# Feed-forward block in two phases through HBM: the first product for all pairs, then the second product with seven block products for eight

## The chip, the cores and the metric

The kernel runs on one core of a Trainium2 chip. A core has TensorE (matrix products, written PE; its weight loads PEld), VectorE (DVE), ScalarE (ACT), GpSimd (POOL) and SyncE (SP), which here issues nearly all transfers (DMAs) between the device memory, HBM, and the on-chip memory, SBUF. Products are summed up in PSUM, eight banks of 128 x 512 float32. The metric is the device time of one execution in microseconds (us).

## What is computed

One layer of a decoder trunk on 1024 tokens of width 1024, in float32. After a mixing part (four groups of token mixers and an output projection) comes the feed-forward block, which the change is about:

```python
    h = h + mixed @ w_out[l]
    f = jnp.square(jax.nn.relu(rms_norm(h, ffn_norm_g[l]) @ w_ff1[l]))   # 1024 -> 4096
    h = h + f @ w_ff2[l]                                                 # 4096 -> 1024
return rms_norm(h, final_norm_g)
```

## The kernel before

**Products in three passes.** Each float32 operand is split into a rounded high part and a low rest (`split`: ScalarE copies and rounds the high part, VectorE subtracts it). A product is three matmuls, high by high, high by low and low by high (`mm3`). `split_to` splits a 128 x 512 piece into one tile of two halves.

**Pairs.** The 4096 columns of the inner layer are taken in 16 pairs of 128-column tiles (`NPAIR`). For a pair, the first product is a matrix of 2 x 2 blocks: two tiles of inner columns by two halves of 512 tokens, summed over two halves of the width. `ff1_pair` computes it with seven block products for eight (Strassen's scheme in Winograd's form): VectorE makes sums of the weight blocks `a11` to `a22`, `mm_half` is one block product of 12 matmuls of 128 x 512, and the banks `ffx`, `ffy`, `ffz`, `ffv` collect them. The operands of the token side (`hb`: `B11`, `B21`, `T1`, `B22`, `T2`, `T3`, `T4`) are made once: `hn_T0` transposes the first half of the tokens, `hn_T1` the second and forms the first sums, `combine_2` and `combine_3` the rest. `add_relu2` adds, applies the squared ReLU and splits the result into `f`.

**Second product.** `ff2` runs right behind, pair by pair and half by half: for each of four token tiles, 2 tiles of inner columns x 2 halves of 512 output columns x 3 passes, 96 matmuls a pair for both halves; `done` adds the result, times the row's norm `rs2`, into `h` on VectorE (128 x 1024). Its weights come through `load_w2`: four pieces of 256 KB a pair through one buffer (tag `e`), each split into `w2h` and `w2l`.

**The first pair** is done in another way (`boot_w`, `boot_t1`, `boot_t2`): eight plain block products, the four of the first token half ahead of `hn_T1`, so that TensorE has work while the second half of the tokens is still being normed and transposed. `h_norm` norms the tiles of `h`: two squares of 512 columns on ScalarE, an addition and a power on GpSimd, a scaling on ScalarE. It is called for the tiles 0 to 3 after the attention's last `attend` of that half, and for 6, 7, 5, 4 after `att_tile(4)`.

**Order.** The program's order and the priorities in it (`tc.high_priority`) are turned by a scheduler into one fixed order for each engine; an instruction or a load goes ahead of its place when its buffers are free in the scheduler's model. At run time each engine, and SP's queue of transfers, works its list strictly in order. Buffers are rings by tag: `w` has ten tiles of 4 KB a partition (split weights), `raw` two (loaded weights), `M` two, `N` and `e` one, `A` eight (the tiles of `h`), `B` eight, `O`, `P`, `K`, `V`, `Z` four each. In PSUM `X` is two tiles of two banks, `W` two banks, `K` and `O` one each.

**The end.** `final` norms a tile of `h` and stores it; the last tile (`final_tile`) goes in pieces of 512, 256 and 256 columns.

## Time and profile before

| | |
|---|---|
| three runs | 1107.32, 1104.01, 1103.83 us; median 1104.01 |
| the profiled execution | 1102.54 us; its span from first to last instruction 1100.8 us |
| mean clock granted to TensorE | 0.979 |
| moved by DMA | 64.99 MB, mean 59 GB/s |
| from the start to 390 us | mixing part, attention, output projections |
| 390 to 455 us | end of the attention, first pair, `hn_T1`: TensorE busy 57.03 of 65.00 us |
| 455 to 1041 us | loop over pairs: TensorE busy 586.00 of 586.00 us, VectorE 384.99, ScalarE 163.98 |
| 1041 to 1101 us | last pair and end: TensorE busy 43.38 of 60.00 us |

How to read the profile: a row of the page's groups gives line, engine, operation, out <- in by the program's names, how often, then busy time and the mean duration of one in ns, then the idle time of the engine before these and what ended it. In the tables by stage a row is a stretch of the span, its length, and the busy us (and number of instructions) of PE, PEld, DVE, ACT, POOL, then the granted clock, the DMA engines' share and GB/s. Matmuls overlap, so the duration of one is more than the time from one to the next.

### The profile page before, as it was taken

To read this page: it belongs to the slowest core of one execution; us is meant where nothing else is said; L and a number is where in the kernel's file an instruction comes from. 1 tells how busy PE (TensorE), PEld (TensorE's weight loads), DVE (VectorE), ACT (ScalarE), POOL (GpSimd) and SP (SyncE) were. 2 spreads that over 40 slices of the span, in tenths; PEclk is the share of its full clock that TensorE was granted. 3 is DMA by queue.
4 is the path that set the end of the run, shared out by engine and by line. 5 is a ranking of instruction groups with operands and counts; after the bars stand their busy time and mean duration, and the time that the engine had idled before them with its cause. 6 is when DMAs were issued, how large, how long until landed. Compare 5 with 4: busy or idle time off the path is not lost.

```text
span 1100.8 us, 12943 instructions
## 1 busy us (share of the span) xinstructions
PE 1042.1 (95%) x4870; PEld 858.5 (78%) x4870; DVE 800.8 (73%) x1096; ACT 430.1 (39%) x805; POOL 174.7 (16%) x217
## 2 busy tenths in 40 slices
PE   9986799999999697999999999999999999999986
PEld 7865688888888585788888888888888888888765
DVE  5999998998797348975667666567567567567557
ACT  7551266546566656241332222322322322322223
POOL 0468756114233210000000000000000000000003
PEclk9998899999999799999999999999999999999998
DMA  9311025011000000121211201202202202202103
GB/s 342 138 51 46 20 71 201 29 39 39 2 22 19 0 7 14 48 67 48 67 41 37 77 18 60 77 10 68 77 10 67 77 10 67 77 10 87 39 29 152
DMA packets 24973, 64.99 MB, mean 59 GB/s; under 512 B 2768, under 2 KB 4688, under 8 KB 24912
## 3 DMA queue, kind: packets, MB, share of 16 engines
q1 hardware_dynamic: 24768, 64.11, 17.2%
q8 instruction: 38, 0.62, 0.2%
q14 instruction: 23, 0.19, 0.1%
q10 hardware_dynamic: 144, 0.07, 0.0%
HBM read 59.97 MB, written 4.19 MB: 58 GB/s over the span
## 4 chain that ended last, share of the span: by engine, by line
PE 74%; DVE 15%; ACT 4%; issue 3%; DMA 3%; POOL 1%; SPq 0%; POOLq 0%; DVEq 0%; ACTq 0%
PE ff L159 29%; PE ffx L159 11%; PE ffy L159 7%; DVE acc L336 7%; PE wo L159 4%; PE ffv L159 4%; PE ffz L159 4%; PE ob L159 2%; PE s L675 2%; PE zc L159 2%; PE zml L159 2%; PE ffb L159 2%; PE woa L159 2%; DMA w_raw<-in_w_ff 1%; PE ptb L718 1%
## 5 line engine op out<-in xcount | busy, mean ns | idle before, releaser
L159 PE MATMUL ff<-w2h,f 128*128 128x512 f32 (+1 forms) x1024 | 336.8, 392 | 11.8 <-ACT w2h L129 4.1
L159 PEld LDWEIGHTS ff<-w2h,f 128*128 128x128 f32 x1024 | 192.3, 188 | 56.8 <-ACT w2h L129 5.4
L949 DVE SCALAR_TENSOR_TENSOR h<-ff,rs,h 128x1024 f32<-128x1024 f32 x127 | 162.1, 1281 | 93.6 <-PE ff L159 92.2
L159 PE MATMUL ff<-w2l,f 128*128 128x512 f32 x512 | 200.2, 391 | 0.0
L159 PE MATMUL ffx<-hnT,w1s 128*128 128x512 f32 x540 | 139.8, 392 | 0.0
L129 ACT ACTIVATE w1s<-w_raw 128x512 fp32r<-128x512 f32 x107 | 67.1, 629 | 159.0 <-PE ffy L159 50.1
L159 PEld LDWEIGHTS ffx<-hnT,w1s 128*128 128x128 f32 x540 | 101.4, 188 | 22.6
L159 PEld LDWEIGHTS ff<-w2l,f 128*128 128x128 f32 x512 | 96.4, 188 | 21.2 <-DVE w2l L130 0.8
L981 POOL TENSOR_SCALAR mr_ms<-mssq,epsr 128x1 f32<-128x1 f32 x7 | 2.7, 392 | 670.5 <-ACT fjunk L979 670.5
L129 ACT ACTIVATE w2h<-w_raw 128x512 fp32r<-128x512 f32 x64 | 40.4, 632 | 163.4 <-PE ff L159 100.2
L130 DVE TENSOR_TENSOR w1s<-w_raw,w1s 128x512 fp32r<-128x512 f32 x107 | 73.3, 687 | 34.4 <-ACT w1s L129 33.0
L336 DVE SCALAR_TENSOR_TENSOR acc<-ycv,cols,acc 128x512 f32<-128x512 f32 (+23 forms) x100 | 96.3, 1002 | 0.8 <-ACT acc L316 0.6
L130 DVE TENSOR_TENSOR w2l<-w_raw,w2h 128x512 fp32r<-128x512 f32 x64 | 44.1, 689 | 65.4 <-ACT w2h L129 65.0
L129 ACT ACTIVATE f<-s 128x512 fp32r<-128x512 f32 x60 | 37.6, 628 | 99.3 <-PE ff L159 59.5
L159 PE MATMUL ffz<-hnT,w1s 128*128 128x512 f32 x180 | 46.7, 393 | 0.0
L130 DVE TENSOR_TENSOR f<-s,f 128x512 fp32r<-128x512 f32 x60 | 41.1, 684 | 7.0 <-ACT f L129 6.8
L159 PE MATMUL ffy<-hnB,w1s 128*128 128x512 f32 x180 | 45.4, 390 | 0.0
L159 PE MATMUL ffv<-hnT,w1s 128*128 128x512 f32 x180 | 44.9, 390 | 0.0
L159 PE MATMUL ffy<-hnT,w1s 128*128 128x512 f32 x180 | 44.5, 393 | 0.0
L159 PEld LDWEIGHTS ffz<-hnT,w1s 128*128 128x128 f32 x180 | 33.8, 188 | 7.8
L159 PEld LDWEIGHTS ffy<-hnT,w1s 128*128 128x128 f32 x180 | 33.8, 188 | 7.7
L849 DVE SCALAR_TENSOR_TENSOR s<-s 128x512 f32<-128x512 f32 x60 | 39.7, 683 | 0.1
(441 smaller groups left out, 1952.0 us busy)
## 6 DMA issues: line engine op xcount, KB each, us to landing
w_raw<-in_w_ff SPq DMA_DIRECT2D x64, 256.0 KB, 2.7
w_raw<-in_w_ff SPq DMA_DIRECT2D x32, 512.0 KB, 4.0
xin<-in_x SPq DMA_DIRECT2D x8, 512.0 KB, 8.4
wo_raw<-in_w_out SPq DMA_DIRECT2D x8, 512.0 KB, 3.6
h<-in_x SPq DMA_DIRECT2D x8, 512.0 KB, 5.7
out<-h SPq DMA_DIRECT2D x7, 512.0 KB, 2.6
xraw<-in_xT SPq DMA_DIRECT2D x8, 256.0 KB, 4.5
xraw<-in_xT SPq DMA_DIRECT2D x4, 512.0 KB, 9.0
```

The lines of the kernel that those rows point to most:

```text
L129: act.activation(h, src, AF.Copy)
L130: dve.tensor_sub(l, src, h.bitcast(F32))
L159: pe.matmul(out, lhs(x), rhs(y), start=start and i == 0, stop=stop and i == 2, skip_group_check=more)
L336: dve.scalar_tensor_tensor(aa, ya, c, aa, ALU.mult, ALU.add)
L675: pe.matmul(sb_[:, c0:c0 + w], q[:, x, qo:qo + P], kt[:, y, 0:w], start=i == 0, stop=i == 2 and not last)
L718: pe.transpose(b[:, place[j] + s * P:place[j] + (s + 1) * P], pts[s][:, (2 * kp + j) * P:(2 * kp + j + 1) * P], ident)
L849: dve.scalar_tensor_tensor(s, s, 0.0, s, ALU.max, ALU.mult)
L949: dve.scalar_tensor_tensor(h[t], banks[t], rs2[:, t:t + 1], h[t], ALU.mult, ALU.add)
L981: pool.tensor_scalar(ms, ssq, 1.0 / D, epsr[:, t:t + 1], ALU.mult, ALU.add)
```

## The change

The feed-forward block is taken apart into three steps. (1) `early(p)`, for pairs 0 to 9: the two block products that need only the first half of the tokens (`B11`, `B21`), 24 matmuls. The first is stored to HBM (`m1`), their sum gives a quarter of `f`; `hn_T1`, `combine_2` and `combine_3` are laced in between. (2) `ff1_pair(p)` for all 16 pairs: pairs 0 to 9 load their first product back and copy it into PSUM, and do the other five block products; pairs 10 to 15 do all seven. Pair 0 is now a pair like the others. `f_out` stores each quarter of `f` to HBM in float32 (`fr`), and three of four also split (`fs`). (3) `ff2_chunk(c)`, four chunks of four pairs: the second product as 2 x 2 blocks (two halves of the tokens, two tiles of inner columns, two halves of the output) with seven block products for eight. A block product (`product`) is 4 token tiles x 4 pairs x 3 passes = 48 matmuls; banks `A` (both `X` tiles) and `B` (`W`, `W`, `K`, `O`) collect them, and after each `add_h` adds the 128 x 512 result to its place in `h`. The sums of the blocks of `f` and `w_ff2` are made by VectorE before products 3 and 4. The operands of products 1, 2 and 7 (`f_load`) come split from HBM into the ring `B`, the others are split from the raw `f` in `K` and `O`; the raw weights lie in `Z` and `P`, the split ones in `w`. `att_h` norms each tile of `h` right behind its `att_tile`, with one square of 1024 columns.

```diff
     with (
...
+        tc.tile_pool(name="hbm", bufs=1, space=bass.MemoryType.DRAM) as hbm,
...
-    ssh = const([P, 2 * NT], "ssh")
+    ssh = const([P, NT], "ssh")
...
     def h_norm(t):
-        for n in range(2):
-            jk = M("hjunk", [512])
-            act.activation(jk, h[t][:, n * 512:(n + 1) * 512], AF.Square, accum_out=ssh[:, n * NT + t:n * NT + t + 1])
-        ms = small(1, "gssq")
-        pool.tensor_tensor(ms, ssh[:, t:t + 1], ssh[:, NT + t:NT + t + 1], ALU.add)
-        power(rs2[:, t:t + 1], ms, 1, "gr", 1.0 / D, nhalf)
+        jk = M("hjunk", [512]).bitcast(BF16)
+        act.activation(jk, h[t], AF.Square, accum_out=ssh[:, t:t + 1])
+        power(rs2[:, t:t + 1], ssh[:, t:t + 1], 1, "gr", 1.0 / D, nhalf)
         act.activation(h[t], h[t], AF.Copy, scale=rs2[:, t:t + 1])
-    HF = (0, 1)
+    def att_h(t):
+        att_tile(t)
+        h_norm(t)
...
+    NEARLY = 10
+    NCH = 4
...
-    def load_w2(p):
...
-    def add_relu2(f, b, s):
...
-    def ring():
...
-    def boot_w():
...
-    def boot_t1():
...
-    def boot_t2():
...
+    def E(name):
+        return sb.tile([P, 512], F32, tag="e", name=name, bufs=1)
+    def dram(name, n, dt=F32):
+        return hbm.tile([P, n], dt, tag=name, name=name, bufs=1)
+    fr = [[dram("fr%d_%d" % (p, i), 1024) for i in range(2)] for p in range(NPAIR)]
+    fs = [{q: dram("fs%d_%d" % (p, q), 1024) for q in (0, 1, 3)} for p in range(NPAIR)]
+    m1 = [dram("m1_%d" % p, 512) for p in range(NEARLY)]
+    def f_out(p, q, b, s, f, stage):
+        dve.tensor_add(f, b, s)
+        dve.scalar_tensor_tensor(f, f, 0.0, f, ALU.max, ALU.mult)
+        nc.sync.dma_start(fr[p][q // 2][:, (q % 2) * 512:(q % 2 + 1) * 512], f)
+        if q != 2:
+            t = split_to(stage("fst"), f)
+            nc.sync.dma_start(fs[p][q], t.rearrange("p x c -> p (x c)").bitcast(F32))
+    def load_w1(p, i):
+        return load_raw(a["w_ff1"][2 * p + i], 1024, "w1_raw")
+    def early(p):
+        ra = load_w1(p, 0)
+        w11 = split_to(slot("w1e"), ra[:, 0:512])
+        w12 = split_to(slot("w1e"), ra[:, 512:])
+        b = W("ffe")
+        mm_half(b, w11, "B11", True)
+        s1 = M("s1e", [512])
+        act.activation(s1, b, AF.Copy)
+        nc.sync.dma_start(m1[p], s1)
+        b = W("ffe")
+        mm_half(b, w12, "B21", True)
+        f_out(p, 0, b, s1, (E, N)[p % 2]("fe"), lambda n: sb.tile([P, 2, 512], F32R, tag="CS", name=n, bufs=1))
     def ff1_pair(p):
-        ra, rb_ = load_w1(p)
+        ra, rb_ = load_w1(p, 0), load_w1(p, 1)
         a11, a12, a21, a22 = ra[:, 0:512], ra[:, 512:], rb_[:, 0:512], rb_[:, 512:]
-        w11 = split_to(ring(), a11)
+        b = X("ffxy")
+        bx, by = b[:, 0:512], b[:, 512:]
+        s1 = E("s1")
+        if p < NEARLY:
+            nc.sync.dma_start(s1, m1[p])
+            if p < 2:
+                pe.matmul(bx, hb["B11", 0][:, 0, 0:P], hb["B11", 0][:, 0, :], start=True, stop=True)
+            act.activation(bx, s1, AF.Copy)
+        else:
+            w11 = split_to(slot("w1s"), a11)
         dve.tensor_add(a21, a21, a22)
         dve.tensor_sub(a11, a21, a11)
-        ws1 = split_to(ring(), a21)
-        bx, by = W("ffx"), K("ffy")
-        mm_half(bx, w11, "B11", True)
-        s1 = M("s1", [512])
-        act.activation(s1, bx, AF.Copy)
+        ws1 = split_to(slot("w1s"), a21)
+        if p >= NEARLY:
+            mm_half(bx, w11, "B11", True)
+            act.activation(s1, bx, AF.Copy)
         mm_half(by, ws1, "T1", True)
         s5 = N("s5")
         act.activation(s5, by, AF.Copy)
-        ws2 = split_to(ring(), a11)
-        w12 = split_to(ring(), a12)
+        ws2 = split_to(slot("w1s"), a11)
+        if p >= NEARLY:
+            w12 = split_to(slot("w1s"), a12)
         dve.tensor_sub(a12, a12, a11)
         mm_half(bx, ws2, "T2", False)
         s2 = M("s2", [512])
         act.activation(s2, bx, AF.Copy)
-        bz, bv = W("ffz"), O("ffv")
-        mm_half(bz, w12, "B21", True)
-        add_relu2(ffw["f", 0, 0], bz, s1)
-        w22 = split_to(ring(), a22)
+        if p >= NEARLY:
+            bz = W("ffz")
+            mm_half(bz, w12, "B21", True)
+            f_out(p, 0, bz, s1, s1, slot)
+        w22 = split_to(slot("w1s"), a22)
         dve.tensor_sub(a22, a11, a22)
+        bv = (K, O)[p % 2]("ffv")
         mm_half(bv, w22, "T4", True)
         s4 = M("s4", [512])
         act.activation(s4, bv, AF.Copy)
-        ws3 = split_to(ring(), a22)
+        ws3 = split_to(slot("w1s"), a22)
         mm_half(bx, ws3, "T3", False)
-        add_relu2(ffw["f", 1, 0], bx, s4)
-        add_relu2(ffw["f", 1, 1], bx, s5)
-        ws4 = split_to(ring(), a12)
+        f_out(p, 1, bx, s4, s4, slot)
+        f_out(p, 3, bx, s5, s5, slot)
+        ws4 = split_to(slot("w1s"), a12)
         mm_half(by, ws4, "B22", False)
-        add_relu2(ffw["f", 0, 1], by, s2)
-    def ff2(hf, fs, last=False):
...
+        f_out(p, 2, by, s2, s2, slot)
+    def f_split(src):
+        return [split_to(unit("B", "fop"), x) for x in src]
+    def w_split(src):
+        return [split_to(slot("w2op"), x) for x in src]
+    def f_load(pp, q):
+        t = [unit("B", "fop") for p in pp]
+        for x, p in zip(t, pp):
+            nc.sync.dma_start(x.rearrange("p x c -> p (x c)").bitcast(F32), fs[p][q])
+        return t
+    def add_h(t, n, b, lo=0, hi=512):
+        hs = h[t][:, n * 512 + lo:n * 512 + hi]
+        dve.scalar_tensor_tensor(hs, b, rs2[:, t:t + 1], hs, ALU.mult, ALU.add)
+    def product(b, fop, wop, start, then, js=range(4)):
+        for j in js:
+            for i in range(NCH):
+                mm3(b[j], lambda x: fop[i][:, x, j * P:(j + 1) * P], lambda y: wop[i][:, y, :],
+                    start and i == 0, i == NCH - 1, not start)
+            then(j)
+    def ff2_chunk(c, last):
+        pp = range(NCH * c, NCH * (c + 1))
+        fu, wu = [], []
+        for p in pp:
+            wu.append([U("ZP"[i], "w2_raw", [2, 512]) for i in range(2)])
+            nc.sync.dma_start(wu[-1][0].rearrange("p x c -> p (x c)"), a["w_ff2"][2 * p])
+        a11 = f_load(pp, 0)
+        for i, p in enumerate(pp):
+            nc.sync.dma_start(wu[i][1].rearrange("p x c -> p (x c)"), a["w_ff2"][2 * p + 1])
+        a12 = f_load(pp, 1)
+        for p in pp:
+            fu.append([U("KO"[i], "f_raw", [2, 512]) for i in range(2)])
+            for i in (1, 0):
+                nc.sync.dma_start(fu[-1][i].rearrange("p x c -> p (x c)"), fr[p][i])
+        b11, b12 = [w[0][:, 0] for w in wu], [w[0][:, 1] for w in wu]
+        b21, b22 = [w[1][:, 0] for w in wu], [w[1][:, 1] for w in wu]
+        f11, f12 = [f[0][:, 0] for f in fu], [f[0][:, 1] for f in fu]
+        f21, f22 = [f[1][:, 0] for f in fu], [f[1][:, 1] for f in fu]
+        xa = [X("ffa") for i in range(2)]
+        A = [xa[j // 2][:, (j % 2) * 512:(j % 2 + 1) * 512] for j in range(4)]
+        B = [W("ffb0"), W("ffb1"), K("ffb2"), O("ffb3")]
+        wop = w_split(b11)
+        product(A, a11, wop, True, lambda j: add_h(j, 0, A[j]))
+        wop = w_split(b21)
+        product(B, a12, wop, True, lambda j: add_h(j, 0, B[j]))
+        t2 = []
+        for i in range(NCH):
+            dve.tensor_sub(f11[i], f11[i], f21[i])
+            dve.tensor_add(f21[i], f21[i], f22[i])
+            dve.tensor_sub(f22[i], f22[i], f11[i])
+            dve.tensor_sub(b11[i], b12[i], b11[i])
+            t2.append(U("V", "t2", [512]))
+            dve.tensor_sub(t2[i], b22[i], b11[i])
+        fop, wop = f_split(f22), w_split(t2)
+        product(A, fop, wop, False, lambda j: add_h(j, 1, A[j]))
+        for i in range(NCH):
+            dve.tensor_sub(f12[i], f12[i], f22[i])
+            dve.tensor_sub(b12[i], b22[i], b12[i])
+            dve.tensor_sub(b21[i], b21[i], t2[i])
+        fop, wop = f_split(f21), w_split(b11)
+        product(B, fop, wop, True, lambda j: add_h(4 + j, 1, B[j]))
+        fop, wop = f_split(f12), w_split(b22)
+        def first(j):
+            add_h(j, 1, B[j])
+            if last:
+                final(j)
+        product(B, fop, wop, False, first)
+        fop, wop = f_split(f11), w_split(b12)
+        product(A, fop, wop, False, lambda j: add_h(4 + j, 1, A[j]))
+        fop, wop = f_load(pp, 3), w_split(b21)
+        def second(j):
+            add_h(4 + j, 0, A[j])
+            if last:
+                final(4 + j)
+        product(A, fop, wop, False, second, range(4 - last))
+        if last:
+            final_tile(fop, wop, A[3])
...
     with tc.high_priority(offset=300):
-        att_tile(0)
...
+        att_h(0)
...
-    with tc.high_priority(offset=2000):
-        for t in range(4):
-            h_norm(t)
-    ff_slots()
-    with tc.high_priority(offset=300):
-        boot_w()
...
+    todo = [lambda j=j: hn_T1(j) for j in range(KH)]
     for j in range(KH):
-        combine_2(j)
-        combine_3(j)
-    ff2(1, f0)
-    for p in range(1, NPAIR):
+        todo.append(lambda j=j: combine_2(j))
+        todo.append(lambda j=j: combine_3(j))
+    for p in range(NEARLY):
+        early(p)
+        if p >= 1:
+            for g in todo[:2 if p > 4 else 1]:
+                todo.pop(0)()
+    for g in todo:
+        g()
+    for p in range(NPAIR):
         ff1_pair(p)
-        load_w2(p)
-        if p == NPAIR - 1:
-            fgain = U("O", "gain_fin", [D])
+    for c in range(NPAIR // NCH):
+        if c == NPAIR // NCH - 1:
+            fgain = sb.tile([P, D], F32, tag="raw", name="gain_fin", bufs=NRAW)
             nc.sync.dma_start(fgain, a["fin_g"].partition_broadcast(P))
-        for hf in HF:
-            ff2(hf, [ffw["f", i, hf] for i in range(2)], p == NPAIR - 1)
+        ff2_chunk(c, c == NPAIR // NCH - 1)
```

All calls of `att_tile` become `att_h`; `ff_slots`, `ff_slots_2`, `load_w2`, `boot_w`, `boot_t1`, `boot_t2`, `add_relu2`, `ff2` and `final_piece` are gone. `final_tile` now has the columns 512 to 1024 of the last tile ready beforehand and does the pieces 0 to 256 and 256 to 512 of product 7.

More of the change, by code (lines that the diff above doesn't have):

```diff
@@ L824, in combine_3 @@
         hb["T4", j] = split_to(unit("P", "hnT4"), raw_b[j])
-    ffw = {}
-    def load_w1(p):
-        return [load_raw(a["w_ff1"][2 * p + i], 1024, "w1_raw") for i in range(2)]
-    def load_w2(p):
-        for i in range(2):
-            wh, wl = ffw["w2", i]
-            for n in range(2):
-                sl = slice(n * 512, (n + 1) * 512)
-                raw = sb.tile([P, 512], F32, tag="e", name="w2_raw", bufs=1)
-                nc.sync.dma_start(raw, a["w_ff2"][2 * p + i][:, sl])
-                split(wh[:, sl], wl[:, sl], raw)
     def mm_half(b, w, name, start):
@@ L862, in ff_slots_2 @@
-    def ff_slots_2():
-        for i in range(2):
-            ffw["w2", i] = [wslot("w2h"), wslot("w2l")]
-        ffw["n"] = 0
-    def ring():
-        ffw["n"] += 1
-        return ffw["ring"][ffw["n"] % 3]
-    boot = {}
-    def boot_w():
-        ra, rb_ = load_w1(0)
-        slots = ffw["ring"] + [ffw["f", 0, 1], ffw["f", 1, 1]]
-        for n, (t, src) in enumerate(zip(slots, (ra[:, 0:512], ra[:, 512:], rb_[:, 0:512], rb_[:, 512:]))):
-            boot[n] = split_to(t, src)
-    def boot_t1():
-        boot["s"] = sb.tile([P, 2, 512], F32, tag="CS", name="boot_s", bufs=1)
-        for i in range(2):
-            b = W("ffb")
-            mm_half(b, boot[2 * i], "B11", True)
-            act.activation(boot["s"][:, i], b, AF.Copy)
-            mm_half(b, boot[2 * i + 1], "B21", False)
-            r = M("r", [512])
-            act.activation(r, b, AF.Relu)
-            dve.tensor_mul(r, r, r)
-            split_to(ffw["f", i, 0], r)
@@ L892, in boot_t2 @@
-    def boot_t2():
-        for i in range(2):
-            b = W("ffb")
-            mm_half(b, boot[2 * i], "T1", True)
-            mm_half(b, boot[2 * i + 1], "B22", False)
-            add_relu2(ffw["f", i, 0], b, boot["s"][:, i])
-        ffw["ring"].append(sb.tile([P, 2, 512], F32R, tag="CS", name="w1s", bufs=1))
+    def E(name):
+        return sb.tile([P, 512], F32, tag="e", name=name, bufs=1)
+    def dram(name, n, dt=F32):
+        return hbm.tile([P, n], dt, tag=name, name=name, bufs=1)
@@ new lines, in final_tile @@
+    def final_tile(fop, wop, b):
+        t = NT - 1
+        jk, ssq, ms = M("fjunk2", [512]).bitcast(BF16), small(4, "lnr_ms"), small(4, "ogs")
+        pieces = [(512, 1024), (0, 256), (256, 512)]
+        for n, (lo, hi) in enumerate(pieces):
+            if n:
+                for i in range(NCH):
+                    mm3(b[:, lo:hi], lambda x: fop[i][:, x, 3 * P:], lambda y: wop[i][:, y, lo:hi],
+                        False, i == NCH - 1, True)
+                add_h(t, 0, b[:, lo:hi], lo, hi)
+            act.activation(jk[:, lo:hi], h[t][:, lo:hi], AF.Square, accum_out=ssq[:, n:n + 1])
+            pool.tensor_scalar(ms[:, n:n + 1], ssq[:, n:n + 1], 1.0 / D, epsr[:, t:t + 1] if n == 0 else ms[:, n - 1:n],
+                               ALU.mult, ALU.add)
+        rs = small(1, "mr_rs")
+        pool.tensor_tensor(rs, ms[:, 2:3], nhalf[:, 0:1], ALU.pow)
+        for lo, hi in pieces:
+            dve.scalar_tensor_tensor(h[t][:, lo:hi], h[t][:, lo:hi], rs, fgain[:, lo:hi], ALU.mult, ALU.mult)
+            nc.sync.dma_start(a["out"][t][:, lo:hi], h[t][:, lo:hi])
@@ L1173, in _trunk @@
     with tc.high_priority(offset=300):
-        att_tile(0)
+        att_h(0)
     with tc.high_priority(offset=2000):
-        att_tile(3)
+        att_h(3)
     attend(0, 2, pts[0, 2])
@@ L1179, in _trunk @@
         pts[1, 2] = scores(1, 2)
-    att_tile(2)
+    att_h(2)
     with tc.high_priority(offset=2000):
@@ L1189, in _trunk @@
     with tc.high_priority(offset=4000):
-        att_tile(1)
+        att_h(1)
     with tc.high_priority(offset=4000):
@@ L1207, in _trunk @@
     with tc.high_priority(offset=1000):
-        att_tile(6)
+        att_h(6)
     attend(3, 2, pts[3, 2])
```

79 lines of the change are left out of this document (6 added, 73 removed).

## The prediction

> **What bounds the kernel now.** First the page: which engine is busy, where, and what the chain of work that ended last is made of.
>
> ```profile
> span 1100.8 us, 12943 instructions
> PE 1042.1 (95%) x4870; PEld 858.5 (78%) x4870; DVE 800.8 (73%) x1096; ACT 430.1 (39%) x805; POOL 174.7 (16%) x217
> PE   9986799999999697999999999999999999999986
> PE 74%; DVE 15%; ACT 4%; issue 3%; DMA 3%; POOL 1%; SPq 0%; POOLq 0%; DVEq 0%; ACTq 0%
> L159 PE MATMUL ff<-w2h,f 128*128 128x512 f32 (+1 forms) x1024 | 336.8, 392 | 11.8 <-ACT w2h L129 4.1
> L159 PE MATMUL ff<-w2l,f 128*128 128x512 f32 x512 | 200.2, 391 | 0.0
> ```
>
> TensorE is busy 95% and 74% of the chain is its own work. The `ff` groups are the second product: 1024 + 512 = 1536 matmuls, and six more on `ff2w`. The 392 ns is a latency (matmuls overlap), so I take the price of one from the chain of waits and the table by stage over three turns of the pair loop:
>
> ```profile
> 1006.91 8.18 PE ff L159 x36
> ```
>
> ```profile
> core 0: us, PE busy (x) PEld busy (x) DVE busy (x) ACT busy (x) POOL busy (x), PEclk, DMA share, GB/s
> 718.45:759.63 41.18, 41.18 (x181) 33.78 (x181) 26.95 (x36) 11.32 (x20) 0.00 (x0) 1.00 0.16 52
> 759.63:800.91 41.28, 41.28 (x182) 33.82 (x181) 27.48 (x36) 11.34 (x20) 0.00 (x0) 1.00 0.16 52
> 370.00:380.00 10.00, 4.61 (x18) 3.56 (x19) 1.27 (x3) 9.94 (x22) 4.30 (x13) 0.55 0.00 0
> 380.00:390.00 10.00, 8.63 (x34) 6.92 (x33) 3.51 (x6) 2.45 (x6) 1.96 (x3) 0.60 0.01 2
> 410.00:420.00 10.00, 7.37 (x40) 5.77 (x38) 5.79 (x10) 8.45 (x16) 1.65 (x5) 1.00 0.19 55
> 420.00:430.00 10.00, 6.43 (x25) 4.19 (x26) 10.00 (x17) 6.17 (x11) 0.00 (x0) 0.83 0.00 0
> 450.00:460.00 10.00, 8.61 (x37) 6.63 (x37) 9.03 (x14) 2.12 (x5) 0.00 (x0) 1.00 0.33 105
> 1041.00:1060.00 19.00, 17.67 (x79) 14.16 (x78) 14.81 (x18) 3.02 (x5) 0.00 (x0) 1.00 0.04 14
> 1060.00:1080.00 20.00, 14.55 (x55) 10.30 (x54) 10.25 (x12) 5.11 (x9) 2.52 (x4) 0.91 0.17 55
> ```
>
> 36 matmuls in 8.18 us: 0.227 us each at full clock. One turn is 84 matmuls of the first product and 96 of the second: 180 x 0.227 = 40.9 of about 41.2 us. TensorE bounds the loop; VectorE has a third of it free, the transfers far more. The other rows show where TensorE is not full: before and during the change from attention to feed-forward (370 to 390, 410 to 430, 450 to 460) and in the last pair (1041 to 1080).
>
> **What goes.** *Matmuls.* Second product: 16 x 96 = 1536 becomes four chunks of 7 products x 4 tiles x 4 pairs x 3 passes = 336, that is 1344. First product: pair 0 loses its eight-product form (96) for seven (84), two dummy matmuls come: -10. Together 202 x 0.227 = **-45.9 us**, all on the path, since TensorE is the chain. The final tile's half-width pieces are as many before as after.
>
> *Old losses.* The pair loop's 41.2 - 40.9 over 15 turns: **-5**. The last pair idles 1.33 + 5.45 us by the last two rows, and its 14.55 busy us at clock 0.91 lose 1.3: **-8**; the second product there waits for weights that pass one buffer (`e`), which no longer exists. Around the boot 2.63 + 3.57 + 1.39 us idle and 1.1 of clock: **-9**; `boot_t1` had run out of matmuls while `hn_T1` was being made, and now ten `early` units, 240 matmuls (54 us), can stand there. The norms: the four first tiles were normed in one lump after the attention, each with two squares; `att_h` norms each tile behind its own output product with one square (on POOL an addition less per tile).
>
> ```profile
> 370.61 3.17 ACT hjunk L755 x10
> ```
>
> ```profile
> 374.87 0.47 PE L788 MATMUL htb<-ident,h 128*128 128x128 f32 x1 [3.92 <-ACT h L759]
> 384.39 0.77 PE L159 MATMUL woa<-wo_0h,oA 128*128 128x512 f32 x1 [1.37 <-DVE hnT L134]
> 384.96 0.63 PE L159 MATMUL woa<-wo_0l,oA 128*128 128x512 f32 x1
> 387.52 0.63 PE L159 MATMUL woa<-wo_0l,oA 128*128 128x512 f32 x1
> ```
>
> ScalarE is full there (9.94 of 10) and TensorE waits 3.92 us for it. Bounds 0 and 5.5 us; attention's other chains are late next, so **-3**. That makes 1102.5 - 45.9 - 5 - 8 - 9 - 3 = 1031.6, if all that is new were hidden.
>
> **What comes.** The new work is on VectorE and in the queues. Its prices:
>
> ```profile
> L130 DVE TENSOR_TENSOR w1s<-w_raw,w1s 128x512 fp32r<-128x512 f32 x92 | 63.2, 687 | 31.8 <-ACT w1s L129 30.5 <-PE ffx L159 0.2
> L129 ACT ACTIVATE w1s<-w_raw 128x512 fp32r<-128x512 f32 x92 | 57.9, 629 | 146.0 <-PE ffy L159 46.1 <-PE ffx L159 34.3 <-DMA w_raw<-in_w_ff 26.1
> ```
>
> ```profile
> 1030.55 0.68 DVE L130 TENSOR_TENSOR f<-s,f 128x512 fp32r<-128x512 f32 x1
> 1033.55 0.68 DVE L849 SCALAR_TENSOR_TENSOR s<-s 128x512 f32<-128x512 f32 x1
> ```
>
> ```profile
> w_raw<-in_w_ff SPq DMA_DIRECT2D x64, 256.0 KB, 2.7
> w_raw<-in_w_ff SPq DMA_DIRECT2D x32, 512.0 KB, 4.0
> out<-h SPq DMA_DIRECT2D x7, 512.0 KB, 2.6
> ```
>
> ```profile
> 0.00:25.00 25.00, 23.22 (x98) 17.71 (x99) 12.91 (x24) 18.93 (x33) 1.51 (x7) 1.00 0.91 341
> ```
>
> ```profile
> 21.62 0.43 SPq L837 DMA_DIRECT2D w_raw<-in_w_ff  x1
> 749.67 32.04 SPq L837 DMA_DIRECT2D w_raw<-in_w_ff  x3
> ```
>
> A VectorE operation on 512 columns lasts 0.69 us, but from 1030.55 to 1033.55 six started in a row: 0.60 apart. A load of 512 KB lands in 4.0 us, a store in 2.6; the most that the transfers moved is 341 GB/s at share 0.91. The last two rows show SP's queue: a weight load of the feed-forward issued at 21.62, far ahead of its place in the program because its buffer was free, and later 32 us in which the queue stood behind one load whose buffer was not. So loads run ahead as far as buffers allow, and one that must wait holds all behind it.
>
> *Early units*, ten: each 24 matmuls (5.4 us), 5 VectorE operations, 0.52 MB loaded and 1.05 stored. `hn_T1` and its combinations (44 operations) lie among them: 94 x 0.60 = 56 us beside 54.4 of matmuls and about 4 of transposes. Transfers: 1.57 MB in about 5.9 us, 266 of 341 GB/s. The loads go through two `raw` buffers shared with `hn_T1`: 4.0 us of load and about 2 of splitting per unit, as long as TensorE's share. Three resources nearly full at once: between 0 (they interleave) and 26 us (a load that takes 6.5 us, so 8.5 per unit), I take **+6**, near the lower end, since VectorE had no gap at 420 to 430 (10.00 of 10).
>
> *First-product phase.* Pairs 0 to 9 have 60 matmuls (13.6 us) and 17 VectorE operations (10.2); pairs 10 to 15 have 84 (19.1) and 22 (13.2). The pair's weights wait for both `raw` buffers: load 4.0, nine operations 5.4, a handover from ScalarE 0.7, 10.1 of 13.6 us, provided that the 8 `f_out` operations (4.8) fall into the load. On SP's queue the three `fr` and two `fs` stores (0.43 us of issue each) wait for VectorE's square, and the next pair's loads can stand behind them; the buffers `M`, `N`, `E` stay taken until their stores have landed (2.6 us), which delays ScalarE's copies of the next pair. From 0 to 3.8 us a pair (all in series: 17.4); before, with 65% of VectorE in use, 0.3 was lost per turn. I take 0.6 x 10 + 0.3 x 6 = **+8**.
>
> *First chunk.* A product is 48 matmuls, 10.9 us. A chunk needs 104 VectorE operations (32 sums, 44 splits, 28 additions into `h`), 63 us of 76; ScalarE 44 x 0.63 = 28. But products 3 and 4 want 48 of the 104 (32 sums, 16 splits). For the first chunk the buffers `P`, `K`, `O` come free in the last pair of the first product, so 12.6 MB (37 us at 341 GB/s) begin some 16 us ahead and end about 21 us in, beside 8 `f_out` operations left over. Before product 3: 46 operations from -2.7 us, 28 us, ready at 25 instead of 21.8; before product 4: 24 to 26 more, ready at 40 instead of 36. **+8**; 0 if the scheduler runs them ahead, 14 if they go at 0.69.
>
> *Later chunks.* `O`, `K`, `Z`, `P` are free from product 4 to 6 on, so the sums run ahead in products 5 to 7, where VectorE has 28 operations of its own (17 us) for 33 us. What cannot run ahead are three groups of 2.1 MB (the `fs` loads of quarters 3, 0 and 1): their eight `B` slots are free only when the product two before ends. Alone each takes 6.2 us at 341 GB/s and some 2.5 of latency of the 10.9; with 8.4 MB of other loads in the same engines it is late. 0 to 8 us a chunk; **4 x 3 = +12**. The last chunk has seven more `final` multiplications (1.2 us each) on VectorE: **+2**. The ends of both kernels after the last matmul are alike: 0.
>
> [...]
>
> Sum: 1031.6 + 6 + 8 + 8 + 12 + 2 = 1067.6. The profiled execution took 1102.54 us, 1.7 beyond its span and 1.5 under the median of the runs, 1104.01. I predict **1068 us**.
>
> After the wait of 3.92 us the clock granted was 0.55, and `woa` matmuls ran at (387.52 - 384.96)/6 = 0.43 us. [...]
>
> **Rivals.** *All hidden*: the scheduler fills every stall but the first chunk's: 1031.6 + 8 = about **1040**. For it: VectorE ran without a gap from 420 to 430, and the queue goes 400 us ahead. Against: VectorE at 75 to 82% in each phase, with its needs in lumps.
>
> *The two raw buffers pace the first product.* Loads take 6.5 us under the stores' traffic (3.15 MB a pair in 13.6 us, 231 of 341 GB/s, in pairs 0 to 9) and part of `f_out` comes after them: 2 us a pair for ten, 0.7 for six, 1.5 for each early unit, 39 instead of 14: **1093**. For it: `raw` and SP's waits behind full buffers; against: 10.1 us of 13.6.
>
> *Each chunk starts cold, slower than before.* SP's queue stands behind the quarter-1 load, which waits for the end of product 7, and the chunk's other loads issue only then. 14.7 MB take 43 us; the first product waits about 14 us, product 3 until 47 (14 + 21.8 = 36 were due), product 4 another 3.5: 28.5 a chunk, 114 over four instead of 20. It decides from (1104 - 1068 + 20)/4 = 14 us a chunk; at full **1160**, halfway 1115. For it: the 32 us row; against: the row at 21.62.
>
> **Chances.** Forecast, 1046 to 1088: 0.62. All hidden: 0.12. Raw buffers: 0.13. Cold chunks: 0.13. The range holds the first three and the edge of the fourth, 1040 to 1103; the likeliest's own is 1046 to 1088. A measurement tells a change from none beyond 0.3% (3.3 us): faster 0.83, within 0.04, slower 0.13.
>
> **What would show it.** 2690 feed-forward matmuls at 0.227 us: right in any case. TensorE full from about 395 to 460: the early units fit; gaps there on `w_raw` speak for the raw buffers. Pairs every 14.2 and 19.4 us in the first phase; chunks every 80 in the second, the first 84, with gaps before products 3 and 4 on VectorE's splits. Wrong: gaps on `fop` loads of over 10 us at each chunk's start, or VectorE waiting in its own queue for TensorE with splits behind.

## The result and the profile after

The change made the kernel slower: 1239.88 us (median of four runs, 1236.93 to 1240.40) against 1105.41 (four runs, 1103.83 to 1107.32), a ratio of 1.121 with a 95% interval of 1.118 to 1.124. The forecast was 1068 us, range 1040 to 1103, with 0.13 for slower.

From the page of the kernel after: its span, the busy times, the granted clock in 40 slices of 31 us, and the shares of the chain by engine.

```profile
span 1237.8 us, 13369 instructions
PE 1074.8 (87%) x4674; PEld 849.9 (69%) x4674; DVE 859.0 (69%) x1312; ACT 483.8 (39%) x898; POOL 177.5 (14%) x209
PEclk9988999999999998888787898888889999999999
PE 51%; DVE 26%; DMA 11%; issue 6%; ACT 4%; POOL 1%; SPq 0%; DVEq 0%; POOLq 0%; ACTq 0%
```

There are 4674 matmuls against 4870: the saving is there (196 in these records, 202 by the forecast's count; the six are the last tile's, which has 24 matmuls of 256 columns here and 12 before). Yet TensorE is busy longer than before, 1074.8 us against 1042.1, while the clock stands at 0.8 and 0.7 in nearly all of slices 16 to 30; and its share of the chain fell from 74 to 51%. Which stage that is, the table by stage of the kernel after tells (stretch, length, busy us of PE, PEld, DVE, ACT, POOL, clock, DMA share, GB/s):

```profile
391.00:466.00 75.00, 61.96 (x263) 46.07 (x261) 57.63 (x93) 39.06 (x66) 1.47 (x4) 0.98 0.56 194
466.00:722.00 256.00, 182.44 (x592) 131.87 (x593) 107.27 (x171) 65.40 (x112) 0.00 (x0) 0.83 0.36 122
722.00:870.00 148.00, 124.16 (x461) 94.36 (x460) 76.12 (x119) 43.48 (x75) 0.00 (x0) 0.87 0.41 146
1037.00:1120.00 83.00, 80.92 (x339) 64.07 (x338) 65.26 (x104) 24.82 (x44) 0.00 (x0) 0.98 0.49 179
```

The forecast's ten pairs at 14.2 and six at 19.4 us make 258 us: counted from 466, where the early units end here, the first product was to end at 724. From 466 to 722, 592 matmuls ran, where 256 us at 0.227 hold 1128; VectorE was busy 107 us, the transfers at 36%. Nothing is full there: everybody waits. A pair of 60 matmuls takes about 25.8 us instead of 14.2, one of 84 takes 27.3 instead of 19.4. The last row is a stretch of the second product: TensorE nearly full. The first matmul of the second product marks the border, and stands at 886.09:

```profile
886.09 0.63 PE L160 MATMUL ffa<-w2op,fop 128*128 128x512 f32 x1
```

So the first product took about 420 us (466 to 886.1) instead of 258: 162 of the 172 us missed. The second product and the end took 1237.8 - 886.1 = 351.7 us; the forecast's chunks of 84 and three times 80, its 2 for the last one and the 8.7 us that follow the last matmul here make 335, 17 less. (That is 7 more than missed in all: the phase began 7 us sooner than the forecast's terms leave room for.)

**Who waits for whom.** The chain of waits of the kernel after, by engine and releaser (us in total, times, longest):

```profile
DVE s L853 <- PE ffxy L160: 177.5, 30, 10.4
ACT fst L130 <- DVE s L854: 93.0, 23, 4.6
PE ffxy L160 <- ACT w1s L130: 82.0, 24, 4.0
```

and one turn of it in the timeline (start, duration, instruction, in brackets the idle time before it and what ended it; `w1s` are split weights, `ffxy` the PSUM tile that holds both bx and by, `s` a result in SBUF, `fst` the split form of a stored quarter, L853 and L854 the sum and the square in `f_out`):

```profile
545.18 5.78 PE L160 MATMUL ffxy<-hnT,w1s 128*128 128x512 f32 x12 [2.68 <-ACT w1s L130]
...
557.39 3.03 PE L160 MATMUL ffxy<-hnT,w1s 128*128 128x512 f32 x12 [0.69 <-ACT s L906]
560.51 1.29 DVE L853 TENSOR_TENSOR s<-ffxy,s 128x512 f32<-128x512 f32 x2 [10.27 <-PE ffxy L160]
561.72 1.28 DVE L854 SCALAR_TENSOR_TENSOR s<-s 128x512 f32<-128x512 f32 x2
...
562.43 1.23 ACT L130 ACTIVATE fst<-s 128x512 fp32r<-128x512 f32 x2 [4.61 <-DVE s L854]
...
563.57 0.61 ACT L130 ACTIVATE w1s<-w_raw 128x512 fp32r<-128x512 f32 x1
...
564.24 4.90 PE L160 MATMUL ffxy<-hnB,w1s 128*128 128x512 f32 x12 [3.82 <-ACT w1s L130]
...
565.02 0.44 SPq L139 DMA_DIRECT2D w_raw<-in_w_ff  x1
...
570.10 0.69 DVE L891 TENSOR_TENSOR w_raw<-w_raw 128x512 f32<-128x512 f32 x1 [0.23 <-DMA w_raw<-in_w_ff]
...
571.51 1.00 PE L160 MATMUL ffxy<-hnT,w1s 128*128 128x512 f32 x2 [2.37 <-ACT w1s L130]
```

Read from the top: T3 runs from 557.39. VectorE has stood idle for 10.27 us for its result, with nothing else allowed ahead of it. Then come sum, square and the split of the two stored quarters, and only then, at 563.57, the split of `ws4`, the weights of the pair's last product B22, whose inputs had been there since before T3. TensorE waits 3.82 us for it. That split also frees the raw buffer: the next load goes out at 565.02, the moment it can, lands at 570, and T1 of the next pair is 2.37 us late. With 0.69 us for a copy these waits are 6.9 us a pair; the granted clock was lower behind the two long ones (T1's twelve matmuls took 5.78 us at 0.50, T3's 3.03 at 1.00). Of the 5 us that are left of the 12 lost in a pair, a mean clock of 0.83 accounts for about 4 (0.17 of 25.8).

### The profile page after: what moved, and what is told of

It reads as the page before. It is cut to its first block, busy times and chain, and to the rows that moved or that the text cites. A ratio compares the mean times of both kernels' runs of the same rounds, so it can differ in the third digit from the quotient of the medians.

```text
span 1237.8 us, 13369 instructions
## 1 busy us (share of the span) xinstructions
PE 1074.8 (87%) x4674; PEld 849.9 (69%) x4674; DVE 859.0 (69%) x1312; ACT 483.8 (39%) x898; POOL 177.5 (14%) x209
## 4 chain that ended last, share of the span: by engine, by line
PE 51%; DVE 26%; DMA 11%; issue 6%; ACT 4%; POOL 1%; SPq 0%; DVEq 0%; POOLq 0%; ACTq 0%
PE ffxy L160 16%; PE ffa L160 8%; DVE acc L337 6%; PE ffb L160 5%; DMA w_raw<-in_w_ff 4%; PE wo L160 4%; PE ffv L160 3%; DMA f_raw<-fr 3%; DVE w2op L131 2%; PE ob L160 2%; PE s L676 2%; DVE s L853 2%; PE zc L160 2%; DVE h L940 2%; PE woa L160 2%
## 5 line engine op out<-in xcount | busy, mean ns | idle before, releaser
L160 PE MATMUL ffxy<-hnT,w1s 128*128 128x512 f32 x648 | 186.6, 439 | 37.3 <-ACT w1s L130 24.7
L160 PE MATMUL ffa<-w2op,fop 128*128 128x512 f32 (+1 forms) x780 | 193.2, 402 | 13.7 <-DVE h L940 10.7
L160 PEld LDWEIGHTS ffxy<-hnT,w1s 128*128 128x128 f32 x648 | 133.3, 211 | 83.3 <-ACT w1s L130 28.8
L160 PEld LDWEIGHTS ffa<-w2op,fop 128*128 128x128 f32 x780 | 147.7, 193 | 55.0 <-DVE h L940 15.6
L853 DVE TENSOR_TENSOR s<-ffxy,s 128x512 f32<-128x512 f32 x48 | 31.7, 687 | 180.8 <-PE ffxy L160 177.5
L160 PE MATMUL ffb<-w2op,fop 128*128 128x512 f32 x576 | 139.1, 396 | 0.0
L160 PE MATMUL ffxy<-hnB,w1s 128*128 128x512 f32 x192 | 77.9, 569 | 63.1 <-ACT w1s L130 57.3
L160 PEld LDWEIGHTS ffb<-w2op,fop 128*128 128x128 f32 x576 | 108.7, 189 | 26.6
L337 DVE SCALAR_TENSOR_TENSOR acc<-ycv,cols,acc 128x512 f32<-128x512 f32 (+22 forms) x100 | 99.0, 1030 | 0.7 <-ACT acc L317 0.4
L940 DVE SCALAR_TENSOR_TENSOR h<-ffa,rs,h 128x512 f32<-128x512 f32 (+1 forms) x65 | 47.8, 737 | 39.3 <-PE ffa L160 39.2
L160 PE MATMUL ffe<-hnT,w1e 128*128 128x512 f32 x240 | 62.6, 409 | 10.3 <-ACT w1e L130 6.5
L131 DVE TENSOR_TENSOR w2op<-w_raw,w2op 128x512 fp32r<-128x512 f32 x96 | 64.9, 681 | 0.6 <-ACT w2op L130 0.6
```

Of the source, the lines that this page charges most:

```text
L131: dve.tensor_sub(l, src, h.bitcast(F32))
L160: pe.matmul(out, lhs(x), rhs(y), start=start and i == 0, stop=stop and i == 2, skip_group_check=more)
L337: dve.scalar_tensor_tensor(aa, ya, c, aa, ALU.mult, ALU.add)
L853: dve.tensor_add(f, b, s)
L940: dve.scalar_tensor_tensor(hs, b, rs2[:, t:t + 1], hs, ALU.mult, ALU.add)
```

## The experiments

All times stand beside runs of the kernel before on the same chip (medians 1103.2 to 1104.7). "Border" is the start of the first matmul of the second product.

| run | us | ratio to before, 95% | border |
|---|---|---|---|
| kernel after | 1239.9 | 1.121 (1.118 to 1.124) | 886.1 |
| e1_ws4_first | 1135.6 | 1.028 (1.025 to 1.031) | 784.2 |
| e2_swap_loads | 1224.6 | 1.109 (1.103 to 1.114) | 868.9 |
| e3_ws4_and_swap | 1130.6 | 1.023 (1.019 to 1.028) | 783.4 |
| e4_third_buffer | 1222.5 | 1.107 (1.102 to 1.111) | 868.4 |
| e5_banks | 1172.2 | 1.062 (1.059 to 1.065) | 823.3 |
| e6_third | 1126.2 | 1.020 (1.018 to 1.023) | 777.2 |
| e7_all | 1169.9 | 1.062 (1.058 to 1.065) | 816.6 |
| e8_warm | 1270.8 | 1.151 (1.149 to 1.154) | 926.0 |
| e11_pool | 1134.3 | 1.027 (1.023 to 1.030) | 786.3 |
| e12_t2pool | 1180.7 | 1.069 (1.065 to 1.072) | 825.0 |
| x2_before_ff1 | 789.0 | 0.714 (0.711 to 0.717) | - |
| r1_ring | 1147.7 | 1.038 (1.032 to 1.044) | 797.4 |
| y1_layout | 1252.1 | 1.134 (1.129 to 1.139) | 898.5 |
| r2_ring_lay | 1090.0 | 0.986 (0.981 to 0.992) | 738.6 |
| r3_both_ring | 1141.1 | 1.032 (1.026 to 1.039) | 790.9 |
| r4_both_ring_lay | 1086.3 | 0.983 (0.977 to 0.989) | 739.4 |
| r4_final | 1088.4 | 0.986 (0.984 to 0.988) | 740.2 |

The total moves with the border: in the kernel after, e3, r1, y1 and r2 what lies behind it is 347 to 352 us of the span. Every run but x2 is thus about the first product's phase.

**Order, buffers or queue?** Three theories: the order of ScalarE's and VectorE's lists keeps `ws4`'s split back; the two raw buffers; SP's queue and the transfers. The edits, in `ff1_pair`:

```diff
+        ws4 = split_to(slot("w1s"), a12)            # e1, e3
         f_out(p, 1, bx, s4, s4, slot)
         f_out(p, 3, bx, s5, s5, slot)
-        ws4 = split_to(slot("w1s"), a12)            # e1, e3
...
-        ra, rb_ = load_w1(p, 0), load_w1(p, 1)      # e2, e3
+        rb_ = load_w1(p, 1)
+        ra = load_w1(p, 0)
```

e4 gives every third load another buffer (tag `CS`).

> In ff1_pair the split of ws4 is traced before the two f_out calls of quarters 1 and 3 instead of behind them. Theory 'order in the queues': in the changed kernel ScalarE and VectorE, which work in order, hold this split behind the two f_out, which wait for product T3; so B22 starts 3.8 us late, both raw buffers come free late, the next pair's T1 waits 2.4 us more, and the gaps halve TensorE's clock for part of each pair. Then this edit alone brings pairs 0 to 9 from 25.8 to about 15 us and pairs 10 to 15 from 27.3 to about 20.5: 1238 - 108 - 41 = about 1090, and the wait on w1s of 82 us falls below 15. Rival 'two raw buffers and the loads' time': only the 3.8 us and their share of the clock go, about 5 us a pair, about 1155. Rival 'stores on SP's queue or transfer rate': no more than 20 us, about 1220.

> In ff1_pair the load of the weights rb_ (blocks a21, a22, which the first sum needs) is traced before that of ra; the order of ws4 and f_out stays as in the changed kernel. The buffer that comes free early (after ws3) then goes to the half that is needed first. Theory 'order in the queues': the 2.4 us before T1 and their share of the clock go, the 3.8 us before B22 stay: about 4.5 us a pair, about 1165. Rival 'two raw buffers and the loads' time': the same or a little more, 1140 to 1165. Rival 'SP's queue or transfer rate': no change, about 1230.

> Both edits: ws4's split before the two f_out, and rb_ loaded before ra. Theory 'order in the queues': as the first edit alone or up to 5 us faster, 1083 to 1092, since the first one already frees both buffers about 8 us before the next pair's T1. Rival 'two raw buffers': clearly faster than the first edit alone, by 30 us or more.

> Nothing moved: the loads of the pairs in ff1_pair go through three buffers instead of two (every third load takes the buffer CS, which only the early units use before). Theory 'order in the queues': the 3.8 us before B22 stay, only the 2.4 us before T1 and their clock share go: about 1165. Rival 'two raw buffers and the loads' time': most of the loss of the first phase goes, pairs at 15 to 17 us, about 1100. Rival 'SP's queue or transfer rate': no change, about 1230.

One line moved up two lines gave 104 us of the miss back; the exchanged loads and the third buffer gave 15 and 17. So the order of the lists is the first cause and the buffers are a small one. e2 and e4 by themselves came out nearest to the number of SP's queue (1230), not to the 1165 of the order; what rules the queue out as the main cause is e1, which it had at 1220. In e2 the wait ahead of T1 went as expected in pairs 0 to 9 (21.8 us a pair instead of 26.0, from one T4 to the next), but pairs 10 to 15 grew from 27.3 to 30.8, as B22's wait did, from 3.82 to 4.7. e3 lies 5 us below e1, as the order had it, and not 30 below, as the raw buffers had it. But e1 stays 45 us above its 1090. The waits of TensorE in e1:

```profile
PE ffxy L160 <- DVE s L853: 24.3, 16, 1.8
```

The wait for the split has gone, and what is late next is B22 again, for another reason. In e3:

```profile
569.29 3.03 PE L160 MATMUL ffxy<-hnB,w1s 128*128 128x512 f32 x12 [1.44 <-DVE s L853]
```

B22 adds into by, and waits for VectorE to read T3's result out of bx: two banks, but one tile of 1024 columns.

**Separate the two halves, add a buffer, fill the gap.** e5 is e3 with `bx, by = X("ffx")[:, 0:512], W("ffy")`; e6 is e3 with the third buffer; e7 has both. e8 is the kernel after with 14 matmuls into an unread bank written between T3 and B22.

> Both moves of the run before it (the split of T3's partner product ahead of the two stores, the load pair exchanged), and the two half tiles bx and by of the first product are two tiles of their own. If the rest of the loss in a pair is B22 waiting until VectorE has read T3's result out of the other half of the same tile (1.44 us in each of pairs 0 to 9, 2.72 us in each of 10 to 15), that wait goes: 14 + 16 = 31 us less than 1130.6, so about 1100. If TensorE then only waits as long for the next thing behind it on VectorE (the sums of the next pair, held by their load), the time stays within 10 us of 1130. The theory of raw buffers expects no change.

> Both moves, and a third buffer for the first product's loads, one tile for both halves as before. With the order mended, the load that VectorE's next sums wait for (about 3.2 us in each of pairs 10 to 15) may now be what counts: then 10 to 20 us less than 1130.6, about 1115. If the shared tile is what B22 waits for, the third buffer gives under 5 us, as it did little without the moves (1222 against 1240).

> Both moves, separate tiles and the third buffer. If each removes its own wait: pairs 0 to 9 at about 14.5 us and 10 to 15 at 20 to 21, against 16.4 and 24.9, so 19 + 26 = 45 us less than 1130.6: about 1086, which is faster than before (1104). If one of the two only uncovers the other, 1095 to 1105, no gain on before. If neither matters, 1125 to 1130.

> The changed kernel as it is, with 14 more matmuls a pair into a bank that nobody reads, standing between T3 and B22, where TensorE waits 3.8 us for the split. No wait of another engine is touched. 14 at 0.227 are 3.2 us. If the lower clock is a large part of a pair's loss (25.8 us where its matmuls need 13.6, with 3.8 + 2.4 + 0.7 us of waits: about 5 us are matmuls at the lower rate), a pair gets about 4 us shorter although it does more: 1170 to 1190. If the clock is only a consequence and the VectorE and ScalarE order alone sets the pace, the time stays within 5 us of 1240; if TensorE's own queue sets it, it rises by 16 x 3.2 = 51 us, to 1290.

e5 was wrong with its sign: 42 us slower than e3. The timeline of e5 shows why:

```profile
555.62 2.88 PE L160 MATMUL ffy<-hnB,w1s 128*128 128x512 f32 x12
558.34 2.88 PE L160 MATMUL ffx<-hnT,w1s 128*128 128x512 f32 x12
...
563.24 1.23 ACT L130 ACTIVATE fst<-s 128x512 fp32r<-128x512 f32 x2
...
564.38 1.65 ACT L130 ACTIVATE w1s<-w_raw 128x512 fp32r<-128x512 f32 x3
...
565.04 1.22 PE L160 MATMUL ffy<-hnT,w1s 128*128 128x512 f32 x2 [3.82 <-ACT w1s L130]
```

With tiles of its own B22 (`hnB`) was ready sooner, the scheduler put it ahead of T3, and now T3 is the pair's last product. Behind it stand the stored quarters again, and behind these the next pair's splits: the same 3.82 us, one product further on. The third buffer is worth 4 us on top of e3 (e6) and 2 on top of e5 (e7, which shares the loss of e5 and missed its 1086).

e8 did not test its question. The scheduler moved the added matmuls: those of pairs 0 to 9 all ran before 519 us, those of pairs 10 to 15 inside other products (below, among those of `ffz`). None stands ahead of B22, whose wait is as long as before:

```profile
678.18 4.35 PE L160 MATMUL ffxy<-hnB,w1s 128*128 128x512 f32 x12 [3.82 <-ACT w1s L130]
...
740.62 3.11 PE L921 MATMUL dummy<-hnT 128*128 128x512 f32 x13
```

So its 31 us do not tell whether matmuls in the gap would pay; that stays open. That the low clock follows from the waits e3 shows: without the two long ones the clock from 466 to 630 us is 0.99, against 0.83 in the kernel after.

**GpSimd for the stored quarters.** e11 is e6 with the low halves of `fst` subtracted on GpSimd; e12 is e7 with that and with T2 ahead of T1.

> Both moves and the third buffer, and the low halves of the stored quarters (two a pair, three in pairs 10 to 15, 0.64 us each on VectorE) are computed on GpSimd. If in the mended order VectorE's list is what holds pairs 10 to 15 (119 of 148 us busy there), at least 6 x 1.9 = 11 us go: 1113 or less against 1126. If only the shared tile of the two products counts (1.44 us at B22), within 3 us of 1126. If GpSimd's work slows VectorE's, longer than 1126.

> As the run before it, and the two halves are tiles of their own again, with T2 now ahead of T1, so that T3 is ready before B22 and the scheduler leaves T3, the product with the two stored results behind it, ahead of B22 in TensorE's list. In the earlier run with separate tiles B22 had gone ahead of T3, and the next pair's T1 waited 3.8 us for a split that stood behind T3's results. If that order was the reason for its 1172, a pair now waits only for the one result of B22 that stands ahead of the next splits (0.69 + 0.68 us) or less: 1095 to 1110. If separate tiles cost for another reason, about 1165 again.

Both missed: 8 us slower than e6, 11 slower than e7. In e12 T3 did stay ahead of B22, and T2 of the next pair still waited 1.10 us for `w1s`; and VectorE's operations took longer while GpSimd worked (its two took 2.98 us together; the square on VectorE beside them, at 540.07, took 1.13 us, and 0.68 in the kernel after, at 544.38):

```profile
539.37 2.98 POOL L859 TENSOR_TENSOR fst<-s,fst 128x512 fp32r<-128x512 f32 x2 [15.02 <-PE ffy L160]
...
540.07 1.13 DVE L854 SCALAR_TENSOR_TENSOR s<-s 128x512 f32<-128x512 f32 x1
...
541.12 2.98 DVE L131 TENSOR_TENSOR w1s<-w_raw,w1s 128x512 fp32r<-128x512 f32 x3
...
574.34 1.78 DVE L131 TENSOR_TENSOR w1s<-w_raw,w1s 128x512 fp32r<-128x512 f32 x1
```

Three splits of VectorE take 2.98 us here and 1.88 without GpSimd's work (a row of r2 below); the whole difference is in the first, which lasts 1.78 us (the row at 574.34, two turns on) and is the only one that overlaps GpSimd's work, up to 542.35.

**Was the second product the cover?** Until here I took it that before the change the second product's matmuls had hidden these waits. x2 takes them away from the kernel before.

> The kernel before with the second product of pairs 1 to 14 left out, its weight loads and splits too (the last pair keeps it). What stays is 84 matmuls a pair, at 0.227 us 19.0 us, in one phase, with nothing stored in HBM and no change of the products. If the matmuls of the second product were the cover that hid the first product's waits, a pair takes 25 to 28 us here too, as in pairs 10 to 15 of the changed kernel (27.3). If the transfers through HBM or the seven-for-eight form make the changed kernel's pairs long, it takes 19 to 20.5 here. Over 14 pairs that are 360 to 390 us against 270 to 285.

That theory fell. Pair after pair of x2:

```profile
512.78:532.00 19.22, 19.22 (x85) 15.75 (x84) 14.44 (x23) 8.85 (x15) 0.00 (x0) 1.00 0.18 55
532.00:551.50 19.50, 19.16 (x84) 15.37 (x84) 13.64 (x23) 8.93 (x15) 0.00 (x0) 1.00 0.19 55
```

The old first product alone takes about 19.3 us a pair at full clock, where the forecast had 19.4 for pairs 10 to 15, with VectorE at about three quarters. So something in the new `ff1_pair` itself keeps the splits back. Of what differs, two things could do it: the old one splits its weights into a ring of three tiles of their own and its results into tiles of their own, where the new one takes both from the ring `w` (`slot`); and the old one has four separate banks, where the new one has bx and by in one tile.

**The ring and the tile.** r1 takes the staging tile of the stored quarters from elsewhere, and moves no line; y1 brings the old layout back; r2 does both; r3 and r4 are r1 and r2 with the two moves of e3.

```diff
+    def fslot(name):                                 # r1 to r4
+        return sb.tile([P, 2, 512], F32R, tag="CS", name=name, bufs=1)
...
-        f_out(p, 1, bx, s4, s4, slot)                # as well for quarters 0 and 3
+        f_out(p, 1, bx, s4, s4, fslot)
...
-        b = X("ffxy")                                # y1, r2, r4
-        bx, by = b[:, 0:512], b[:, 512:]
+        bx, by = W("ffx"), (K, O)[p % 2]("ffy")
...
-        bv = (K, O)[p % 2]("ffv")
+        bv = (O, K)[p % 2]("ffv")
```

> The changed kernel with one thing changed: the staging tiles of the stored quarters (fst) of the first product's pairs come from the single tile of tag CS, no longer from the ring w that the split weights come from. No line is moved. Theory of the ring: tiles of one ring are given out in the program's order, so ws4's tile can't be given out before those of the two stored quarters, which wait for T3; that is why ws4's split stands behind them in the lists of ScalarE and VectorE. With a tile of their own the scheduler puts the split ahead by itself, and the time falls as it did when the split was moved by hand (1135.6) or further: 1090 to 1140. If the order came from elsewhere or a single staging tile holds everything up: 1200 or more.

> As the run before it, and the first product's PSUM tiles are laid out as in the kernel before: bx in W, by and bv in K and O in turn, none sharing a tile. If the shared tile costs 1.44 us a pair at B22 once the order is mended, about 14 + 16 = 30 us less than the run before it. If the scheduler's other order makes a wait elsewhere, as with the earlier separate tiles (1172), within 10 us of it or more.

> Both moves by hand (split ahead, load pair exchanged; 1130.6) and the staging tile of its own. If the ring had kept other splits back too (those of the next pair stand behind the stored quarters as well), 1090 to 1115; if ws4's was the only one that counted, 1125 to 1135.

> Both moves, the staging tile and the layout of the kernel before. By the theory that order and shared tiles are all that is lost in the first product, a pair takes what it took in the kernel before without its second product: 14.5 us for pairs 0 to 9, 19.3 for 10 to 15, against 16.4 and 24.9: 1130 - 19 - 34 = 1077, faster than before. If they only trade one wait for another, 1110 to 1170.

> The changed kernel with the old layout of the first product's PSUM tiles (bx in W, by and bv in K and O in turn) and nothing else; the staging tiles stay in the ring w. The fourth corner of the square: ring alone gave 1147.7, ring and layout 1090.0, neither 1239.9. If the ring's order is the first cause and the layout only shows once it is mended, ws4's split still stands behind the stored quarters and the time stays above 1200. If the two add, 1239.9 - 57.7 = 1182. If the layout alone is enough, 1100 to 1150.

> The kernel of r4_both_ring_lay once more, for the interval: 1084 to 1089, a ratio to before of 0.981 to 0.986. It leaves nothing out. If the first time was chance, 1095 or more.

Of these forecasts y1's and that of the repeated r4 came in. r1 lies 8 us above its range, r2 fell by 58 us where 30 were expected, r3 got longer, and r4 is 9 above its 1077. But the square is closed: neither 1239.9, layout alone 1252.1, ring alone 1147.7, both 1090.0. The layout costs 12 us where the ring is as it was and brings 58 where it is mended. y1 still has the old wait, r1 has not; there each of the three waits below is for work on the other half of the shared tile: the copy of by, the copy into bx, the sum that reads bx (the rows of y1 and of r1):

```profile
PE ffy L160 <- ACT w1s L130: 88.8, 25, 3.8
```

```profile
PE ffxy L160 <- ACT s L902: 16.3, 5, 6.6
PE ffxy L160 <- ACT ffxy L891: 11.9, 6, 2.6
PE ffxy L160 <- DVE s L856: 8.7, 7, 2.0
```

In r2 the splits stand where their inputs are ready (timeline around a T3; L905 and L914 are two of the next pair's sums of weight blocks), and the first product's phase is nearly full (table by stage):

```profile
652.72 1.14 ACT L130 ACTIVATE w1s<-w_raw 128x512 fp32r<-128x512 f32 x2
652.80 1.88 DVE L131 TENSOR_TENSOR w1s<-w_raw,w1s 128x512 fp32r<-128x512 f32 x3
653.11 2.88 PE L160 MATMUL ffx<-hnT,w1s 128*128 128x512 f32 x12
654.61 0.68 DVE L905 TENSOR_TENSOR w_raw<-w_raw 128x512 f32<-128x512 f32 x1
655.21 0.68 DVE L914 TENSOR_TENSOR w_raw<-w_raw 128x512 f32<-128x512 f32 x1
...
655.92 1.16 ACT L130 ACTIVATE w1s<-w_raw 128x512 fp32r<-128x512 f32 x2 [2.06 <-DVE w_raw L914]
656.03 1.29 DVE L856 TENSOR_TENSOR s<-ffx,s 128x512 f32<-128x512 f32 x2
...
658.60 0.63 ACT L130 ACTIVATE fst<-s 128x512 fp32r<-128x512 f32 x1 [1.52 <-issue]
```

```profile
466.00:722.00 256.00, 247.51 (x1054) 197.18 (x1055) 181.82 (x293) 108.20 (x188) 0.00 (x0) 0.99 0.57 201
```

1054 matmuls instead of 592 in the same stretch, 8.5 us of it idle. The splits at 652.72 and 655.92 are already those of the next pair, at 655.92 its `ws3` and `ws4`. Both begin before the sums that read T3's result (656.03; T3 is the row at 653.11), and the stored quarter's split comes after them, at 658.60: it no longer holds them back. The two moves add little to that: r4 is 3.7 us below r2, within their intervals. So r2 and r4 are faster than both kernels, if by little against the one before: r4, measured once more, takes 1088.4 us, 0.986 of before (0.984 to 0.988) and 12% under the kernel after.

Why would the staging tiles hold a split back? The two ways that mend it say that it is the order in which the ring's tiles are given out: e1 moves the split's line ahead of the stored quarters and leaves the ring alone; r1 takes the quarters out of the ring and leaves the lines alone. Each alone removes the wait (all but 0.6 us in e1 and 4.8 in r1 of 82.0), and e1 leaves the number of tiles and of their users as it was. That the scheduler gives out the tiles of one ring in the program's order I infer from this; I have not shown it inside the scheduler.

## Why the prediction was wrong, point by point

- **The terms that went.** -45.9 for 202 matmuls: the count is right. The price is right for the first product; in the second a matmul takes (1073.20 - 1070.40)/12 = 0.233 us instead of 0.227, 8 us over 1344 of them:

```profile
1070.40 2.96 PE L160 MATMUL ffb<-w2op,fop 128*128 128x512 f32 x12
1073.20 2.03 PE L160 MATMUL ffa<-w2op,fop 128*128 128x512 f32 x8
```

  What makes them longer stays open. The old losses (-25 in all) were not measured one by one.
- **Early units, +6: too low, but within the 0 to 26.** TensorE was busy 61.96 of the 75 us to 466, so 13 were idle. In that part 6.5 us went by ahead of matmuls that wait for the split weights (`w1e`), and ScalarE waited 11.3 us for the loads behind them: the gaps that the forecast named as speaking for the raw buffers.
- **First-product phase, +8: the step that failed.** It cost 162 us more than forecast (the border at 886 instead of 724). Its bounds were 0 to 3.8 us a pair, "all in series", and that was no upper bound (nor does the text add up to its 17.4: 4.0 + 5.4 + 0.7 + 4.8 are 14.9, and 17.5 with a store's 2.6): it counted the loads and VectorE's operations of one pair, and asked whether they fit into the matmuls' time. They do: VectorE was busy 107 of 256 us. What it did not ask is where in ScalarE's and VectorE's fixed lists each split stands, and so whom it waits for. The provision was there in the text, "provided that the 8 `f_out` operations (4.8) fall into the load": `ws4`'s split stood behind them, and they behind T3. Freeing the staging tiles from the ring gave 92 us back. Nor did it ask what it costs that bx and by now lie in one tile: 58 us once the ring is mended. The sum itself, with its 0.6 x 10 + 0.3 x 6, is 5 us short of what the phase costs without these two: r2 is idle for 8.5 us up to 722 and for 4.7 more up to 740, behind its border.
- **First chunk, +8: too small; later chunks, +12: about right.** The first chunk's 336 matmuls took 98.8 us up to the start of the second chunk (886.1 to 984.9), where the forecast has 84; the clock was 0.91 there, and ten matmuls of the last pair stood among them. The next two took 82.7 and 82.1 us where it has 80, and the 0.233 us a matmul are 2 of the difference. With the failed step mended the span of r2 is 1087.0 us, still 21 above the forecast's 1066, 13 of it behind the border (348.3 against 335).
- **The rivals.** The raw buffers had the place right and the cause and the size wrong: a third buffer gave 17 of the miss. Cold chunks, the one rival for slower, did not happen: it had 28.5 us lost in each chunk, and the later ones lost 2 to 3 against the forecast. The case that happened was none of them, though the last line of what would show a wrong forecast names it: VectorE waiting in its own queue for TensorE with splits behind.
- **Taking the loop apart.** That is not what made the kernel slower: x2 needs nothing interleaved to run at 19.3 us a pair, and r2 and r4 are taken apart in the same way and are faster than the interleaved kernel. In r2 TensorE is the busiest in both phases (247.51 of 256 us in the first, 78.57 of 82 in a chunk of the second).
- **The clock.** The forecast saw 0.55 granted behind a wait of 3.92 us in the kernel before, and has no term for the clock in the first product. After the waits of 3.82 and 2.37 us the clock granted was 0.50 for 3.4 us each time (from 564.96 and from 571.78), 0.83 on average over the phase, and the twelve matmuls behind the first took 4.90 us. Behind the shorter wait it was as low as behind the longer.

What stays open besides the 0.233 us: why e11, e12 and r3 lie above the kernels that they were built on by 8 to 11 us. For e11 and e12 VectorE's longer operations beside GpSimd's, as e12's trace has them (1.78 us for a split), are a likely part; for r3 it may be the single staging tile, for which ScalarE waits in r1, r2 and r4 (39.2, 36.3 and 35.7 us). Neither was isolated.
